# Scales for the up weights found unit by unit, the second norm's weight applied at the transposed eviction, two surveys moved

## The chip, the core and the metric

The kernel runs on one core of a Trainium2 chip. That core has a matrix engine (TensorE, PE in the rows), three engines for elementwise work (VectorE or DVE, ScalarE or ACT, GpSimd or POOL), and SyncE (SP), which here does little but issue transfers. Each engine works through its own queue in order; they meet by semaphores. The metric is the device time of one execution in microseconds (us).

## The reference

The kernel computes one layer of an encoder on 1024 positions of width 1024, in fp32:

```python
h = layer_norm(x, ln_in_w, ln_in_b)
h = layer_norm(DN_ALPHA * h + hybrid_mixer(h, ...), ln1_w, ln1_b)
h = layer_norm(DN_ALPHA * h + memory_xattn(h, mem, w_xq, w_xkv, w_xo, b_xo), ln2_w, ln2_b)
h = layer_norm(DN_ALPHA * h + conv_ffn(h, w_up, b_up, w_dw, b_dw, w_down, b_down), ln3_w, ln3_b)
```

`hybrid_mixer` is one input projection, a bidirectional chunked mLSTM on half of its columns and a neighbourhood attention on the rest, and an output projection. `memory_xattn` attends from each position to 256 memory tokens in four heads. `conv_ffn` multiplies by `w_up` (1024 x 5632) and adds `b_up`, applies a depthwise convolution of width 3 over positions, gates one half of the columns with the GELU of the other, and multiplies by `w_down` (2816 x 1024).

## The kernel before

**Numbers.** Each fp32 operand of a matmul is split into an f16 high and an f16 low part, and `mm3` (L217 to L219) adds three matmuls: high with high and the two mixed ones. So that the parts fit f16's range, an operand is first multiplied by a power of two. For a weight that power comes from a *survey*: the matrix is loaded once just to be measured (`survey_gen`, L194 to L206: an Abs on ScalarE with a running sum at L205, for a few pieces a maximum on VectorE at L203), `scale_of` (L168 to L177) folds the sums into one number for all partitions with a small matmul (the bank `mx`, L174) and `pow2` makes the power of two and its inverse. Later the weight is loaded again, piece by piece, and split by `split16` (L189 on ScalarE, L190 on VectorE). The survey of `w_up` is 44 loads of 512 KB, that of `w_down` 11 of 1 MB, those of `w_xo` and `w_xq` four of 1 MB each.

**Stages**, with their places in the profiled span. *Stage A* (0 to 200 us): input norm, and the columns of the input projection that are wanted with positions on partitions (`tk`, L323); its loop steps the surveys of `w_down`, `w_xo`, `w_xq`. *Mixer* (200 to 640): the other columns, mLSTM and neighbourhood attention. *Output projection and first norm* (640 to 690): `out_half` makes one tile of 128 positions after the other, `after1` (L928 to L936) normalises it, stores it to `h1_d`, steps the survey of `w_up` and, three tiles later, `to_T16` transposes it into f16 operands. `ln_tile` (L226 to L244) is the norm: VectorE statistics, GpSimd power (L235), ScalarE (r - mean)/std (L241), VectorE times weight (L242), GpSimd plus bias (L243). *Cross-attention* (690 to 900): queries (`xq`), then per head scores `S`, softmax (L1039 to L1044: maximum, difference, exponential, sum, normalisation), transposes of the probabilities (L1047), `PTh`/`PTl` and `pv`; between its steps, queries of later heads and the survey. *Second projection and norm* (840 to 955): `out_d` loads the residual tile `r` (`load_r`, which also adds `b_xo / ALPHA` on GpSimd, L1094), adds the projection, normalises, stores to `h2_d`; `to_B` (L982 to L1010) transposes it with TensorE (L989) and makes the f16 operands of the feed-forward: B11, B21, B22 and the sums T1 to T4. *Feed-forward up* (1000 to 1440): 22 units of 256 columns, gate and value half, each seven products of 12 matmuls in place of eight (a Strassen scheme): A11, A12, A22 and sums S1 to S4 of the unit's weight blocks against B and T. `Units.load` and `prep` bring and split a unit two units ahead, into one of four *homes* (buffers named `unitYh`, `unitYl`, `unitA`, `whi`/`wlo` in the rows) by the one scale `su`. `take` (L1267) empties a product's bank: m1, u2, u3, C21 by ScalarE with the bias, C11, C22, C12 by VectorE adding a kept piece. `post` (L1242) does convolution, GELU, gate and the store. *Down projection and third norm* (1360 to 1625).

**What sets the order.** All engines' queues are laid out ahead by the tile framework, which simulates the program on a timeline and picks the next instruction; within a queue nothing overtakes. SyncE issues nearly all loads and stores, one after the other, and a load whose buffer isn't free yet holds those behind it. Buffers of one name rotate in program order. The few lines on the old survey of `w_up`:

```python
survey = survey_gen(sv, [(I["w_up"][i // 2, :, i % 2 * 1024:i % 2 * 1024 + 1024], i) for i in range(2 * NFF)])
...
run(survey)
pu, su = scale_of(sums[:, 0:2 * NFF], 13)
```

## Time and profile before

| What | Value |
|---|---|
| three timed runs | 1631.69, 1631.81, 1634.49 us; median 1631.81 |
| profiled execution | 1627.17 us, span 1625.5 us |
| TensorE busy | 1503.0 us, 92% of the span |
| VectorE, ScalarE, GpSimd busy | 973.4, 753.2, 544.6 us |
| moved by DMA | 226.69 MB, mean 139 GB/s |

The profile is of one execution. The rows are of these kinds. A *window* gives, for a stretch of the span, each engine's busy time with its count of instructions, then TensorE's granted clock as a share of full speed (PEclk), the busy share of the DMA engines and what they moved. A *wait* row names who waited for whom, the total, how often, and the longest. A *group* row gives line, engine, operation, output and inputs, shapes, the count, busy time and mean ns of one, then the engine's idle time before them and what ended it. A *timeline* row gives start, duration, the instruction and, in brackets, the idle time before it and what ended that. `SPq` is the queue of loads and stores.

### The profile page before, as it was taken

To read this page: it belongs to the slowest core of one execution; us is meant where nothing else is said; L and a number is where in the kernel's file an instruction comes from. 1 tells how busy PE (TensorE), PEld (TensorE's weight loads), DVE (VectorE), ACT (ScalarE), POOL (GpSimd) and SP (SyncE) were. 2 spreads that over 40 slices of the span, in tenths; PEclk is the share of its full clock that TensorE was granted. 3 is DMA by queue.
4 is the path that set the end of the run, shared out by engine and by line. 5 is a ranking of instruction groups with operands and counts; after the bars stand their busy time and mean duration, and the time that the engine had idled before them with its cause. 6 is when DMAs were issued, how large, how long until landed. Compare 5 with 4: busy or idle time off the path is not lost.

```text
span 1625.5 us, 21513 instructions
## 1 busy us (share of the span) xinstructions
PE 1503.0 (92%) x8112; PEld 975.5 (60%) x8112; DVE 973.4 (60%) x1719; ACT 753.2 (46%) x1258; POOL 544.6 (34%) x372
## 2 busy tenths in 40 slices
PE   6998999999888989797789968999999999999997
PEld 5998888889777878644345533444444444444443
DVE  7411611237578885767566786887777676835333
ACT  3335201225555765656654444656665655622111
POOL 5414222114457761322002546454345410010133
PEclk9999999999999999898989978999999999999999
DMA  8278511266556325777631313222222232741112
GB/s 299 91 270 299 172 52 59 97 169 177 161 163 214 132 79 187 254 261 255 220 130 39 114 68 107 84 98 91 99 83 78 91 130 78 281 146 53 62 55 78
DMA packets 80377, 226.69 MB, mean 139 GB/s; under 512 B 7824, under 2 KB 26512, under 8 KB 76048
## 3 DMA queue, kind: packets, MB, share of 16 engines
q1 hardware_dynamic: 80128, 224.82, 40.3%
q8 instruction: 64, 1.05, 0.3%
q0 software_dynamic: 144, 0.49, 0.2%
q14 instruction: 41, 0.34, 0.1%
HBM read 182.71 MB, written 43.06 MB: 139 GB/s over the span
## 4 chain that ended last, share of the span: by engine, by line
PE 59%; DMA 12%; DVE 9%; ACT 6%; POOL 5%; issue 4%; SPq 0%; POOLq 0%; ACTq 0%; DVEq 0%
PE z L217 7%; PE z L218 7%; PE z L219 7%; PE dn L218 4%; PE dn L219 4%; PE dn L217 4%; DMA sv<-in_w_up_dram 4%; PE cl L217 4%; PE cl L219 4%; PE cl L218 4%; DMA whi<-mrow 2%; DMA mo<-ev 1%; ACT sv L205 1%; DMA r<-h 1%; PE o L863 1%
## 5 line engine op out<-in xcount | busy, mean ns | idle before, releaser
L127 POOL TENSOR_TENSOR wlo<-wraw,whi 128x1024 fp32r<-128x1024 f32 (+1 forms) x36 | 86.8, 2416 | 193.6 <-ACT whi L126 184.2
L190 DVE SCALAR_TENSOR_TENSOR wlo<-wraw,sc,whi 128x1024 f16<-128x1024 f32 x67 | 87.8, 1319 | 83.8 <-ACT whi L189 83.6
L217 PE MATMUL dn<-whi,yp 128*128 128x512 f16 x336 | 127.2, 379 | 0.0
L218 PE MATMUL dn<-wlo,yp 128*128 128x512 f16 x336 | 127.2, 379 | 0.0
L219 PE MATMUL dn<-whi,yp 128*128 128x512 f16 x336 | 126.9, 379 | 0.0
L189 ACT ACTIVATE whi<-wraw,sc 128x1024 f16<-128x1024 f32 x67 | 75.8, 1144 | 105.4 <-PE dn L219 46.3
L235 POOL TENSOR_TENSOR lnrs<-lnrs,mhalf 128x1 f32<-128x1 f32 x32 | 26.3, 822 | 283.9 <-DVE lnrs L234 161.6
L126 ACT ACTIVATE whi<-wraw 128x1024 fp32r<-128x1024 f32 (+1 forms) x48 | 50.4, 1056 | 121.8 <-PE cl L218 75.4
L205 ACT ACTIVATE sv<-sv 128x1024 f32<-128x1024 f32 (+1 forms) x55 | 70.9, 1289 | 71.8 <-DMA sv<-in_w_down_dram 38.3
L1173 POOL TENSOR_TENSOR wraw<-ur 128x512 f32<-128x512 f32 x22 | 41.2, 1873 | 156.1 <-DVE wlo L190 73.6
L243 POOL TENSOR_TENSOR r<-r,vec 128x1024 f32<-128x1024 f32 x22 | 51.8, 2356 | 77.5 <-DVE r L242 69.4
L1434 POOL TENSOR_TENSOR r<-r,vec 128x1024 f32<-128x1024 f32 x8 | 19.0, 2376 | 158.2 <-ACT r L1433 158.2
L1250 DVE SCALAR_TENSOR_TENSOR cbuf<-C,wdw,cbuf 128x1024 f32<-128x1024 f32 x44 | 70.7, 1607 | 1.1
L217 PEld LDWEIGHTS <-whi 128*128 128x128 f16 x364 | 36.3, 100 | 56.5 <-issue 16.5
L1249 DVE SCALAR_TENSOR_TENSOR cbuf<-C,wdw,cbuf 128x1024 f32<-128x1024 f32 x44 | 63.7, 1448 | 7.7 <-ACT cbuf L1248 6.7
L218 PEld LDWEIGHTS <-whi 128*128 128x128 f16 x364 | 36.2, 99 | 47.7 <-issue 7.7
L219 PEld LDWEIGHTS <-wlo 128*128 128x128 f16 x364 | 36.1, 99 | 45.1 <-issue 3.6
L217 PE MATMUL tk<-whi,X2h 128*128 128x256 f32 (+1 forms) x192 | 56.2, 292 | 6.5 <-DVE ev L323 5.2
L1248 ACT ACTIVATE cbuf<-C,bdw,wdw 128x1024 f32<-128x1024 f32 x44 | 54.4, 1236 | 12.2 <-DVE C L1286 11.4
L219 PEld LDWEIGHTS <-yp 128*128 128x128 f16 x352 | 34.4, 98 | 41.5
L217 PEld LDWEIGHTS <-yp 128*128 128x128 f16 x352 | 34.4, 98 | 41.5
L218 PEld LDWEIGHTS <-yp 128*128 128x128 f16 x352 | 34.4, 98 | 41.4
(444 smaller groups left out, 4850.9 us busy)
## 6 DMA issues: line engine op xcount, KB each, us to landing
sv<-in_w_up_dram SPq DMA_DIRECT2D x44, 512.0 KB
ur<-in_w_up_dram SPq DMA_DIRECT2D x22, 1024.0 KB
r<-h SPq DMA_DIRECT2D x23, 512.0 KB
sv<-in_w_down_dram SPq DMA_DIRECT2D x11, 1024.0 KB
y<-cbuf SPq DMA_DIRECT2D x22, 512.0 KB
ur<-y SPq DMA_DIRECT2D x11, 1024.0 KB
wraw<-in_w_down_dram SPq DMA_DIRECT2D x22, 512.0 KB
wraw<-in_w_col_dram SPq DMA_DIRECT2D x16, 512.0 KB
```

Source lines behind the costliest of these rows:

```text
L126: A.activation(hi[:, :n], r3, AF.Copy)
L127: (eng or G).tensor_tensor(lo[:, :n], r3, hi[:, :n].bitcast(F32), OP.subtract)
L189: A.activation(hi, src, AF.Copy, scale=s)
L190: V.scalar_tensor_tensor(lo, src, s, hi, op0=OP.mult, op1=OP.subtract)
L205: A.activation(t, t, AF.Abs, accum_out=sums[:, i:i + 1])
L217: T.matmul(ps, lh, rh, start=first, stop=False, skip_group_check=skip)
L218: T.matmul(ps, lh, rl, start=False, stop=False, skip_group_check=skip)
L219: return T.matmul(ps, ll, rh, start=False, stop=last, skip_group_check=skip)
L243: G.tensor_tensor(r, r, b_t, OP.add)
L1248: A.activation(c, C[:, 1:SEQ + 1], AF.Identity, scale=wdw[:, 1, j:j + 1], bias=bdw[:, j:j + 1])
L1249: V.scalar_tensor_tensor(c, C[:, 0:SEQ], wdw[:, 0, j:j + 1], c, op0=OP.mult, op1=OP.add)
L1250: V.scalar_tensor_tensor(c, C[:, 2:SEQ + 2], wdw[:, 2, j:j + 1], c, op0=OP.mult, op1=OP.add)
```

## The change

Line numbers of the changed kernel differ from those above; both stand in the rows below.

1. The survey of `w_up` is gone: 44 loads, 40 Abs and 4 maxima. In its place each unit is measured from the copy that is loaded anyway: `bound` runs one Abs over its 128 x 2048 values (output dumped into the unit's own home, sum kept), `scale` folds the sums with one bf16 matmul into `mx`, a reduction and four tiny VectorE operations. The unit's scale `c` is then applied where a product leaves its bank (`take`), so m1, u2, u3 are written straight into the convolution's buffers `C`, and VectorE's additions become (product x c + piece).
2. The survey of `w_down` leaves stage A. It becomes 22 loads of 512 KB, written in the source inside the feed-forward loop (`survey_down`), into two buffers that hold the second norm's weight and bias before. In stage A the other eight loads come at every fourth tile.
3. The second norm's weight and bias no longer pass through `ln_tile` (no L242, L243 for its eight tiles; for the last tile one VectorE operation in place of two). They are applied in `to_B` at the transposed eviction, where a column of 128 is one partition's constant: eight ScalarE operations of 128x128 with scale and bias columns (`wb2`) in place of two of 128x512. The stored residual is without them; the end stage multiplies and adds them there.
4. `b_xo / ALPHA` is added on GpSimd in the first norm's stage (`to_h1`, after the transposes, before the store to `h1_d`), no longer in `load_r`.
5. At the end `r` is scaled and shifted by two GpSimd operations instead of one ScalarE and one GpSimd.
6. Unit 0 is prepared after the second step of the second half of `out_d`, part of unit 1 (A11, A12, A22) between its tiles, the rest of unit 1 in the loop's first round.

The core of the diff:

```diff
+    def amax_all(am, b, idt):
+
+        pb = bank("mx")[:, :128]
+        T.matmul(pb, bass.AP(tensor=am.tensor, offset=am.offset, ap=[am.ap[0], [0, 128]]), idt, start=True, stop=True)
+        V.tensor_reduce(b, pb, axis=mybir.AxisListType.X, op=OP.max)
...
+        if late and w_t is None:
+            return V.tensor_scalar(r, r, mv[:, 0:1], rs[:, 0:1], op0=OP.subtract, op1=OP.mult)
...
-                survey = survey_gen(sv, [(I["w_down"][g], 22 + g) for g in range(NFF // 2)] + [
+                survey = survey_gen(sv, [
                     (I["w_xo"][256 * i:256 * i + 256].rearrange("(a p) c -> p a c", a=2), 33 + i) for i in range(4)] + [
-                    (I["w_xq"][2 * i:2 * i + 2].rearrange("i p k c -> p i (k c)"), 16 + i) for i in range(4)])
+                    (I["w_xq"][2 * i:2 * i + 2].rearrange("i p k c -> p i (k c)"), 16 + i) for i in range(4)], range(16, 20))
...
-                        if tt % 2 == 0 or c > 3:
+                        if tt % 4 == 0:
...
-        survey = survey_gen(sv, [(I["w_up"][i // 2, :, i % 2 * 1024:i % 2 * 1024 + 1024], i) for i in range(2 * NFF)])
...
+            bxo = vec(2, "b_xo")
+            V.tensor_scalar(bxo, bxo, 1.0 / ALPHA, None, op0=OP.mult)
+
+            def to_h1(tt, r):
+                to_T16(r, h1, tt, s1)
+                G.tensor_tensor(r, r, bxo, OP.add)
+                S.dma_start(h1_d[tt * 128:(tt + 1) * 128, :], r)
...
-                next(survey, None)
                 rq.append((tt, r))
                 if len(rq) > LAG:
-                    t_, r_ = rq.pop(0)
-                    to_T16(r_, h1, t_, s1)
+                    to_h1(*rq.pop(0))
...
+            B1 = B1s[:, tt // 2]
+            if tt % 2:
+                dst = [r[:, i * 512:i * 512 + 512].rearrange("p (k t) -> p k t", k=4) for i in range(2)]
+            else:
+                dst = [B1[:, q] for q in range(2)]
+            for q in range(2):
+                for k in range(4):
+                    i = 4 * q + k
+                    A.activation(dst[q][:, k], pts[q][:, k], AF.Identity, scale=wb2[:, i:i + 1], bias=wb2[:, 8 + i:9 + i])
...
-                    A.activation(B1[:, q, :, o], pts[q], AF.Copy, scale=sh)
-                    A.activation(Bh[:, 0, q, :, o], B1[:, q, :, o], AF.Copy)
-                    V.tensor_tensor(Bh[:, 1, q, :, o], B1[:, q, :, o], Bh[:, 0, q, :, o], OP.subtract)
+                    A.activation(Bh[:, 0, q, :, o], B1[:, q], AF.Copy)
...
-            A.activation(e12, pts[0], AF.Copy, scale=sh)
-            A.activation(e22, pts[1], AF.Copy, scale=sh)
+            e12, e22 = dst
...
+            wb2 = small.tile([128, 16], F32, name="wb2")
+            S.dma_start(wb2, I["ln2_c"])
+            V.tensor_scalar(wb2, wb2, sh, None, op0=OP.mult)
...
-                    G.tensor_tensor(rs[tt], rs[tt], bxo, OP.add)
...
-        run(survey)
-        pu, su = scale_of(sums[:, 0:2 * NFF], 13)
...
+            def bound(self, v):
+
+                if v < NFF:
+                    self.am[v] = ur.tile([128, 1], BF, name="am", tag="am", bufs=3)
+                    l1 = ur.tile([128, 1], F32, name="l1", tag="l1", bufs=3)
+                    A.activation(self.home(v)[1].bitcast(BF), self.raw[v], AF.Abs, accum_out=l1)
+                    V.tensor_copy(self.am[v], l1)
+
+            def scale(self, v):
+                if v < NFF:
+                    b = ur.tile([128, 4], F32, name="us", tag="us", bufs=5)
+                    self.s[v] = b[:, 2:3], b[:, 3:4]
+                    amax_all(self.am.pop(v), b[:, 0:1], identb)
+                    pow2(b[:, 0:1], 14, (b[:, 1:2], b[:, 2:3]))
...
+        out_d2 = out_d(range(4, NT), "out", 1)
+        next(out_d2)
+        units.bound(0)
+        units.bound(1)
+        next(out_d2)
+        units.scale(0)
+        units.scale(1)
         run(units.prep(0))
-        out_d2 = out_d(range(4, NT), "out", 1)
-        for _ in range(9):
+        for _ in range(4):
             next(out_d2)
-        run(units.prep(1))
         units.load(2)
+        prep1 = units.prep(1, True)
+        next(prep1)
+        for _ in range(3):
+            next(out_d2)
+        next(prep1)
         run(out_d2)
+        units.bound(2)
...
-                    A.activation(m1, X[v], AF.Identity, bias=bg)
+                    A.activation(g0, j4(X[v]), AF.Identity, scale=c, bias=bg)
                 elif what == "C11":
-                    V.tensor_tensor(g0, j4(Z[v]), j4(m1), OP.add)
+                    V.scalar_tensor_tensor(g0, j4(Z[v]), c, g0, op0=OP.mult, op1=OP.add)
...
+            def survey_down(i):
+
+                t = sv[i % 2]
+                S.dma_start(t, I["w_down"][i // 2, :, i % 2 * 1024:i % 2 * 1024 + 1024])
+                A.activation(t, t, AF.Abs, accum_out=dsum[:, i:i + 1])
...
+                units.scale(v + 2)
...
+                if v < NFF - 1:
+                    survey_down(v)
+                    if v == 0:
+                        survey_down(NFF - 1)
+                units.bound(v + 3)
...
-                A.activation(r, r, AF.Copy, scale=al)
-                G.tensor_tensor(r, r, bd, OP.add)
+                G.tensor_tensor(r, r, rw, OP.mult)
+                G.tensor_tensor(r, r, rb, OP.add)
```

**SyncE's queue in the first norm.** Before, survey loads (`sv<-in_w_up`) stand between the residual's loads and stores and the query weights (`wraw<-in_w_xq`):

```order
L730 DMA r<-part_73 128x1024 x4
L199 DMA sv<-in_w_up_dram 128x1024 x3
L930 DMA h_74<-r 128x1024
L199 DMA sv<-in_w_up_dram 128x1024 x2
L730 DMA r<-part_73 128x1024
L930 DMA h_74<-r 128x1024
L199 DMA sv<-in_w_up_dram 128x1024 x3
L930 DMA h_74<-r 128x1024
L199 DMA sv<-in_w_up_dram 128x1024 x2
L133 DMA wraw<-in_w_xq_dram 128x1024
```

Of the change, from the same place on to the start of cross-attention:

```order
L934 DMA h_74<-r 128x1024
L133 DMA wraw<-in_w_xq_dram 128x1024 x2
L1030 DMA wraw<-xk 128x2x256
L934 DMA h_74<-r 128x1024
L1031 DMA wraw<-xv 128x2x256
L1030 DMA wraw<-xk 128x2x256
L1031 DMA wraw<-xv 128x2x256
L934 DMA h_74<-r 128x1024 x2
L114 DMA vec_7858<-in_ln_w_dram 128x1024
L934 DMA h_74<-r 128x1024
L1325 DMA sv_9201<-in_w_down_dram 128x1024
L114 DMA vec_7860<-in_ln_b_dram 128x1024
```

No survey load is left in the first norm. All 22 of `w_down` (L1325) follow from here on, though the source has them in the feed-forward loop: their buffers are free once the second norm's weight and bias have been measured.

**TensorE between the second projection and the feed-forward** (`out`: the projection's products; `tp`: transposes of the normalised tiles; `z`: feed-forward products). Before, eight transposes stand well inside the projection, and sixteen behind its last matmul:

```order
L219 MATMUL out<-whi,pYl 128x512
L989 MATMUL tp<-ident,r 128x128 x8
L217 LDWEIGHTS pYl
...
L219 MATMUL out<-whi,pYl 128x512
L989 MATMUL tp<-ident,r 128x128 x16
L217 LDWEIGHTS unitYh
L217 MATMUL z<-Bh,unitYh 128x512
```

Of the change:

```order
L219 MATMUL out<-whi,pYl 128x512
L172 LDWEIGHTS am
L172 MATMUL mx<-identb,am 128x128
L993 MATMUL tp<-ident,r 128x128 x40
L217 LDWEIGHTS unitYh
L217 MATMUL z<-Bh,unitYh 128x512
```

The transposes of five tiles (3 to 7) now stand together behind the last matmul, after unit 1's `mx`.

**ScalarE behind the projection, of the change** (L1169: Abs of a unit; L193: split of a unit; L1003: evictions of transposes with the norm's weight and bias; L1019: f16 copies of T operands):

```order
L1169 ACTIVATE unitYl,l_9103<-ur 128x2048
L1003 ACTIVATE r<-tp,wb_7868 128x128 x8
L193 ACTIVATE unitA<-ur,us 128x1536
L1003 ACTIVATE Bf<-tp,wb_7868 128x128 x3
L1019 ACTIVATE TX1l<-wraw 128x4x128
```

Before, tile 3's evictions were two operations and no Abs stood ahead of them.

116 lines of the change are left out of this document (57 added, 59 removed).

## The prediction

> **What bounds the kernel now.** I read the page first: busy shares, then the chain that ended last.
>
> ```profile
> PE 1503.0 (92%) x8112; PEld 975.5 (60%) x8112; DVE 973.4 (60%) x1719; ACT 753.2 (46%) x1258; POOL 544.6 (34%) x372
> PE z L217 7%; PE z L218 7%; PE z L219 7%; PE dn L218 4%; PE dn L219 4%; PE dn L217 4%; DMA sv<-in_w_up_dram 4%; PE cl L217 4%; PE cl L219 4%; PE cl L218 4%; DMA whi<-mrow 2%; DMA mo<-ev 1%; ACT sv L205 1%; DMA r<-h 1%; PE o L863 1%
> ```
>
> TensorE is busy for 1503.0 of 1625.5 us, so a change that leaves its matmuls alone can win at most its 122.5 us of idleness and what the reduced clock costs. The chain names a removed transfer: the survey of `w_up` holds 4% of it (some 65 us, much of which other work would hold in its stead), and its Abs (L205) 1%. The next view, ten-microsecond windows, tells where TensorE loses.
>
> ```profile
> core 0: us, PE busy (x) PEld busy (x) DVE busy (x) ACT busy (x) POOL busy (x), PEclk, DMA share, GB/s
> 150.00:160.00 10.00, 8.14 (x68) 7.72 (x66) 2.06 (x9) 5.65 (x8) 4.89 (x5) 1.00 0.97 329
> 160.00:170.00 10.00, 6.03 (x28) 6.03 (x29) 6.11 (x18) 2.84 (x4) 1.54 (x2) 0.50 0.85 308
> 680.00:690.00 10.00, 3.00 (x11) 2.00 (x12) 6.80 (x11) 7.50 (x12) 0.55 (x1) 0.61 0.87 291
> 700.00:710.00 10.00, 7.33 (x30) 3.34 (x29) 7.64 (x11) 6.20 (x9) 1.99 (x3) 0.83 0.83 263
> 730.00:740.00 10.00, 4.03 (x19) 2.45 (x18) 8.64 (x16) 7.12 (x14) 2.41 (x2) 0.67 0.94 363
> 740.00:750.00 10.00, 5.95 (x28) 3.95 (x28) 9.73 (x20) 4.23 (x12) 6.88 (x3) 0.67 0.52 210
> 770.00:780.00 10.00, 4.64 (x30) 2.96 (x29) 4.99 (x9) 6.75 (x14) 0.00 (x0) 0.89 0.80 263
> 960.00:970.00 10.00, 3.06 (x14) 2.39 (x13) 8.65 (x11) 5.17 (x6) 5.52 (x3) 0.50 0.25 100
> 970.00:980.00 10.00, 7.31 (x19) 2.47 (x19) 9.56 (x13) 4.00 (x7) 6.12 (x3) 0.54 0.19 67
> 1059.00:1240.00 181.00, 181.00 (x840) 82.09 (x839) 143.38 (x114) 108.76 (x122) 85.03 (x42) 1.00 0.24 88
> ```
>
> Ten units of the feed-forward loop (last row, 18.1 us each) leave TensorE no gap at full clock: nothing can be won there, only lost. The losses that this change touches lie at four places: around 160 us (end of stage A), 680 to 710 (tail of the first norm), 730 to 780 (start of cross-attention) and 955 to 1000 (second norm into the feed-forward). Third view, waits:
>
> ```profile
> PE tk L217 <- DVE ev L323: 5.2, 1, 5.2
> ACT sv L205 <- DMA sv<-in_w_up_dram: 27.1, 20, 3.7
> SPq L199 <- ACT sv L205: 67.8, 32, 7.1
> PE tp L989 <- POOL r L243: 10.0, 2, 6.0
> PE pv L217 <- ACT PTh L189: 6.1, 2, 5.4
> ```
>
> The second and third rows (640 to 850 us) are head-of-line blocking both ways: ScalarE stands 27.1 us for survey data with norm and softmax work queued behind, and the load queue stands 67.8 us for ScalarE with real loads behind.
>
> **The change part by part**, against the profiled execution's own 1627.17 us.
>
> *Stage A.* 11 of 19 MB of surveys leave. The `tk` wait of 5.2 us is for an eviction whose buffer a store still held, at a moment with the DMA at 0.97. The windows 150 to 170 lack 1.86 + 3.97 = 5.8 us of matmul, and 6.03 us at clock 0.50 cost 3.0 more. With 8 MB left the queue has room: I take −6; bounds 0 (the other 8 MB fill it as well) and −9.
>
> *Tail of the first norm, 680 to 710.* In 680 to 690 and 700 to 710, 7.0 + 2.7 us are idle, and clocks of 0.61 and 0.83 cost 1.2 + 1.2. The last tiles' norm stands behind surveys on ScalarE:
>
> ```profile
> 677.81 1.06 ACT L205 ACTIVATE sv<-sv 128x1024 f32<-128x1024 f32 x1 [1.96 <-DMA sv<-in_w_up_dram]
> 681.52 1.04 ACT L205 ACTIVATE sv<-sv 128x1024 f32<-128x1024 f32 x1
> 683.13 1.05 ACT L205 ACTIVATE sv<-sv 128x1024 f32<-128x1024 f32 x1
> 686.77 1.15 ACT L189 ACTIVATE whi<-wraw,sc 128x1024 f16<-128x1024 f32 x1 [2.50 <-DMA wraw<-in_w_xq_dram]
> ```
>
> Three Abs with a wait of 1.96 make 5.1 us, and the weight that comes 2.50 us late was queued behind survey loads. All go: 7.6 us, plus a third of the clock's loss: −9. Bounds −13 (idleness and clock whole) and −4. The eight `b_xo` adds that move into this stage are on GpSimd, which has room (0.55 of 10 in the window 680 to 690); what they may do to VectorE is a rival below.
>
> *Start of cross-attention, 730 to 750.* The removed adds of `load_r` ran here, and VectorE's smallest work waited for them:
>
> ```profile
> 737.59 9.29 POOL L1094 TENSOR_TENSOR r<-r,vec 128x1024 f32<-128x1024 f32 x4 [14.28 <-DMA r<-h]
> 738.34 1.68 DVE L1040 TENSOR_TENSOR mn<-mn,sc 128x1 f32<-128x1 f32 x2
> 740.00 2.25 DVE L1040 TENSOR_TENSOR mn<-mn,sc 128x1 f32<-128x1 f32 x1
> 742.42 2.26 DVE L1044 TENSOR_SCALAR P<-P,mn 128x256 f32<-128x256 f32 x1
> 744.79 2.25 DVE L1044 TENSOR_SCALAR P<-P,mn 128x256 f32<-128x256 f32 x1
> 747.62 0.27 DVE L1040 TENSOR_TENSOR mn<-mn,sc 128x1 f32<-128x1 f32 x2
> 748.33 0.35 DVE L1044 TENSOR_SCALAR P<-P,mn 128x256 f32<-128x256 f32 x1
> ```
>
> The last two rows show the same operations undisturbed. The four slow rows exceed them by 1.4 + 2.1 + 1.9 + 1.9 = 7.3 us, on the softmax chain for which TensorE waits (10.0 us idle in the two windows). With a little of the clock's 3.3 us: −8; bounds −12 and −2 (the first scores wait for their operands anyway).
>
> *Rest of cross-attention.* The moved survey of `w_down`, 22 loads of 512 KB, lands exactly here by the order of the load queue, where 21 of `w_up` stood. Each costs ScalarE the same 1.05 us. So the 5.4 us wait for `PTh` and the window 770 to 780 largely stay: −2; bounds −8 and +4 (blocking at another softmax step).
>
> *Second norm into the feed-forward.*
>
> ```profile
> 959.12 1.97 PE L989 MATMUL tp<-ident,r 128*128 128x128 f32 x8 [3.98 <-POOL r L243]
> 972.08 0.58 PE L217 MATMUL z<-Bh,unitYh 128*128 128x512 f16 x1 [2.99 <-ACT Bh L994]
> 994.29 0.58 PE L218 MATMUL z<-TX1l,unitYh 128*128 128x512 f16 x1 [1.78 <-DVE TX1l L1010]
> 443.53 1.28 ACT L538 ACTIVATE whi<-whi,g_sb 128x128 f32<-128x128 f32 x4 [3.06 <-DMA whi<-mrow]
> L189 ACT ACTIVATE unitA<-ur,sc 128x1536 f16<-128x1536 f32 x6 | 9.4, 1565 | 1.8 <-PE z L218 1.8
> L205 ACT ACTIVATE sv<-sv 128x2048 f32<-128x2048 f32 x15 | 28.7, 1914 | 44.5 <-DMA sv<-in_w_down_dram 38.3 <-DMA sv<-in_w_xo_dram 6.2
> L1009 ACT ACTIVATE TX1h<-wraw 128x512 f16<-128x512 f32 x8 | 4.9, 624 | 3.8 <-DVE wraw L1006 2.0 <-DVE wraw L1004 1.8
> L993 ACT ACTIVATE Bf<-tp,sc 128x512 f32<-128x512 f32 x8 | 5.1, 679 | 1.6 <-PE tp L989 1.6
> ```
>
> Now: the projection ends at 959.12 − 3.98 = 955.1, the first feed-forward product starts 16.9 later, and the T-operand products run for good from 994.3, 39 later. After: the GpSimd add and the multiply leave the norm, but the order puts the transposes of tiles 3 to 7 behind the last projection matmul, and an eviction becomes eight pieces: 2 × 1.28 = 2.6 us a tile for 2 × 0.68. ScalarE then does, in its queue's order up to the first B operand, an Abs (1.9 + 0.2 for its read-out), tile 3 (2.6), a split (1.6), tiles 4 to 6 (7.7), nine T copies between them (9 × 0.62) and three f16 copies (3 × 0.68): 21.6, less some 0.09 by which neighbours overlap (four of 0.39 took 1.28) on a dozen of them: 20.5 us to the first product, 3.6 later than now. The 48 B products take 48 × 0.216 = 10.4 (181.0 us for 10 × 84 gives 0.216), and with a third of them at half clock, as now, 14: to 34.5. The T operands of the last tile are done within that. So 35 to 37 against 39, and 1.7 less in the projection, whose last sixteen transposes moved out (8 took 1.97 at the reduced clock): −5. Bounds: −13 (the waits of 10.0 and half the clock) and +6 (evictions at 0.39 us a piece instead of 0.32, with the T operands behind them).
>
> *Feed-forward loop.* Per unit: one more matmul, one more Abs and a little on VectorE.
>
> ```profile
> L174 PE MATMUL mx<-ident,sc x16: 271/275/275, 365.5 to 1477.9; 128*128 128x128 f32 x16
> ```
>
> ScalarE has 108.76/10 = 10.9 us a unit and gets 2.1 more, VectorE 14.3 and about 1 more (six tiny operations; the scaled evictions are the same in number and size): both stay under 18.1. On TensorE 22 matmuls of at most 0.27 us, whose form is cheaper than this f32 one: +2; bounds +1 and +6. A cover gone is the slower rival.
>
> *End.* The scaled residual becomes two GpSimd operations of 2.4 us for a ScalarE one and one:
>
> ```profile
> L1434 POOL TENSOR_TENSOR r<-r,vec 128x1024 f32<-128x1024 f32 x8 | 19.0, 2376 | 158.2 <-ACT r L1433 158.2
> ```
>
> GpSimd stood idle 158 us around its eight; 19 more hide under the projection: 0; bounds 0 and +2.
>
> **Sum:** −6 − 9 − 8 − 2 − 5 + 2 + 0 = −28, 1599 for the profiled execution. The median lies 4.6 above it (1631.81): **1604**.
>
> **Rivals.**
> *The blocking moves with the survey.* The queue order speaks for it: 22 loads, two buffers, in-order Abs between softmax steps. Then cross-attention gains nothing (8 + 2 lost) and its delay eats the junction's 5: 1631.8 − 6 − 9 + 2 = 1619. Against it: the four rows at 738 to 747 owe nothing to a survey.
> *The lock moves with the add.* Eight adds of 2.6 us enter the first norm's stage. If each holds VectorE for 2.1, as the row at 740.00 did, that is 17 us of VectorE in a stage where this row has it busy 32 of 50:
>
> ```profile
> sum 50.00, PE 40.36 PEld 32.71 DVE 32.24 ACT 27.54 POOL 12.28; mean PE 8.07 PEld 6.54 DVE 6.45 ACT 5.51 POOL 2.46
> ```
>
> (640 to 690.) It would be full, and the gain of 9 gone: 1613. The Trainium skill (SBUF — State Buffer, section "SBUF: two separate sides") states a mechanism for this: a GpSimd operation and a VectorE operation with two SBUF inputs exclude each other for the whole instruction. The rows at 738 and 740 agree (two-input L1040); the one-SBUF-input L1044 at 742.42 was held as well, which that sentence alone allows only in a fast mode. Against the rival, without the page: a held VectorE hurts only on the last two tiles, before them the projection covers it.
> *More goes.* Without both causes cross-attention's start and the idleness at 770 vanish whole, each term at its good bound but the loop: 1631.8 − 9 − 13 − 12 − 8 − 13 + 2 ≈ 1579.
> *Slower: the loop falls out of step.* The Abs writes its dump into the next unit's buffer, so in ScalarE's queue it waits until TensorE has left that buffer; behind it stand u3's and the next m1's evictions, for which the product's PSUM bank waits. Between m1 and the product's next use lie 24 matmuls, 5.2 us. If the Abs makes m1 later than that, by 1.6 us say (a wait of 4.7 and its 2.1), 22 units pay 35: 1604 + 35 = 1639. Against: 7 us a unit free on ScalarE; for: one strict queue.
>
> **How the numbers follow.** Forecast 0.57, own range 1592 to 1615; blocking moves 0.18; the lock 0.08; more goes 0.08; out of step 0.06; the parts cancel 0.03. Range 1579 to 1624, which leaves out the last two and little more. 0.2% (3.3 us) is about what a measurement tells from no change: faster 0.57 + 0.18 + 0.08 + 0.08 = 0.91, same 0.03, slower 0.06.
>
> **What would show it.** Stage A: no `tk` wait near 160 and a clock of 1.00. First norm: 680 to 690 with TensorE above 6. Cross-attention: L1050 and L1054 (the softmax lines now) at 0.15 to 0.5 us; Abs (L1325) waits on ScalarE of 10 us and more mean the blocking rival. Junction: one long TensorE wait of 17 to 21 us before the first `z` and a second product group without its 4.5. Loop: 18.1 to 18.3 us a unit. A unit above 18.5, or POOL adds (L933) beside 2 us DVE rows after 675, would make me wrong.

## The result, and the profile after

| | Before | Changed |
|---|---|---|
| median of the timed runs | 1631.75 us (1629.98 to 1634.49) | 1615.32 us (1612.37 to 1616.35) |
| ratio, 95% interval | 1 | 0.9895 (0.9876 to 0.9914) |
| profiled execution, span | 1627.17, 1625.5 us | 1615.6, 1613.9 us |

The change makes the kernel faster: by 1.05% by the ratio, whose interval leaves out 1, and by 16.4 us between the medians. 1604 was forecast, 27.8 us less. The two profiled executions lie 11.6 us apart, since that of before was 4.6 us faster than its median and that of after was not; the account below is made between the two profiles.

First the page of the changed kernel (engines, then the lines of the chain that ended last):

```profile
PE 1497.6 (93%) x8132; PEld 969.9 (60%) x8132; DVE 980.9 (61%) x1836; ACT 763.9 (47%) x1284; POOL 544.8 (34%) x373
DVE cbuf L1284 4%; DVE cbuf L1285 3%; DVE wlo L194 2%; DMA sv<-in_w_down_dram 2%; PE z L217 2%; PE out L217 2%; PE z L219 2%; PE z L218 2%; PE out L219 2%; PE out L218 2%; DMA r<-h 2%; ACT whi L193 1%; POOL r L247 1%; DVE unitYl L194 1%; POOL r L1486 1%
```

The survey of `w_up` has left the chain; in its place stand a survey again (that of `w_down`) and VectorE's convolution steps of the feed-forward loop. The windows, at the places of the prediction:

```profile
160.00:170.00 10.00, 8.98 (x75) 8.72 (x74) 9.09 (x21) 1.17 (x3) 2.22 (x3) 1.00 0.40 134
670.00:680.00 10.00, 3.14 (x19) 2.70 (x18) 9.64 (x11) 4.72 (x7) 6.66 (x2) 0.81 0.44 157
720.00:730.00 10.00, 1.27 (x6) 0.49 (x5) 4.76 (x10) 4.30 (x9) 2.35 (x1) 0.70 0.64 199
730.00:740.00 10.00, 4.70 (x24) 3.05 (x24) 4.82 (x13) 6.99 (x14) 0.00 (x0) 0.62 0.92 343
950.00:960.00 10.00, 4.79 (x18) 3.19 (x19) 7.27 (x10) 10.00 (x27) 2.75 (x3) 0.50 0.00 0
1079.00:1264.60 185.60, 182.56 (x844) 81.00 (x843) 153.68 (x172) 127.96 (x141) 78.85 (x40) 1.00 0.23 85
```

The hole at 160 us is nearly closed. The hole in the first norm's tail is still there (now at 670, 3.14 us of matmul where 3.00 was), and at the start of cross-attention TensorE does 1.27 + 4.70 us of work in 20. The last row holds ten units of the feed-forward loop: they take 185.6 us, not 181.3. What TensorE waits for (640 to 760 us, then 1010 to 1480):

```profile
PE S L217 <- ACT kh L193: 11.9, 1, 11.9
PE tp L266 <- POOL r L247: 6.9, 1, 6.9
...
PE mx L172 <- DVE am L1170: 2.5, 4, 0.8
```

In the profile of before (640 to 760 us) the wait for `kh` is 2.4 us, the first norm's tail waits for something else, a step of its statistics, and there is no wait for a unit's `mx`:

```profile
PE tp L262 <- DVE lnrs L234: 5.3, 1, 5.3
PE S L217 <- ACT kh L189: 2.4, 1, 2.4
```

To see what each is worth, the span was cut at first and last starts of groups of matmuls, whose amount of work the change hardly alters (`cl`: the mixer's first products; `od` and `out`: the second projection's, of the first and the second half of the positions):

| Stretch on TensorE, us | before | changed | difference | forecast |
|---|---|---|---|---|
| start to first `cl` (stage A) | 178.9 | 171.8 | −7.1 | −6 |
| to last mixer output product (mixer) | 499.4 | 498.9 | −0.5 | 0 |
| to first `od` (first norm's tail, cross-attention) | 167.7 | 161.9 | −5.8 | −19 (9 + 8 + 2) |
| to last `out` of the second projection | 108.8 | 106.8 | −2.0 | −1.7 |
| to last `z` with `TX1l` (junction and loop) | 426.3 | 427.2 | +0.9 | −1.3 |
| to the end | 244.4 | 247.3 | +2.9 | 0 |
| sum | 1625.5 | 1613.9 | −11.6 | −28 |

Behind the last `z` with `TX1l` 24 more `z` products follow, among the first products of the down projection. One line of the table carries most of the error: 13 us of the 19 that the first norm and cross-attention should have given did not come.

### The profile page after: what moved, and what is told of

The parts are those of the page before. It is cut to its first block, busy times and chain, and to the rows that moved or that the text cites. A ratio compares the mean times of both kernels' runs of the same rounds, so it can differ in the third digit from the quotient of the medians.

```text
span 1613.9 us, 21573 instructions
## 1 busy us (share of the span) xinstructions
PE 1497.6 (93%) x8132; PEld 969.9 (60%) x8132; DVE 980.9 (61%) x1836; ACT 763.9 (47%) x1284; POOL 544.8 (34%) x373
## 3 DMA queue, kind: packets, MB, share of 16 engines
q8 instruction: 64, 1.05, 0.3%
## 4 chain that ended last, share of the span: by engine, by line
DVE 22%; PE 20%; ACT 11%; issue 9%; DMA 9%; POOL 6%; POOLq 0%; SPq 0%; ACTq 0%; DVEq 0%
DVE cbuf L1284 4%; DVE cbuf L1285 3%; DVE wlo L194 2%; DMA sv<-in_w_down_dram 2%; PE z L217 2%; PE out L217 2%; PE z L219 2%; PE z L218 2%; PE out L219 2%; PE out L218 2%; DMA r<-h 2%; ACT whi L193 1%; POOL r L247 1%; DVE unitYl L194 1%; POOL r L1486 1%
## 5 line engine op out<-in xcount | busy, mean ns | idle before, releaser
L1203 POOL TENSOR_TENSOR wraw<-ur 128x512 f32<-128x512 f32 x22 | 44.6, 2028 | 195.0 <-issue 184.2
L243 ACT ACTIVATE r<-r,lnrs 128x1024 f32<-128x1024 f32 x22 | 27.3, 1240 | 148.7 <-DVE lnrs L242 148.7
L1284 DVE SCALAR_TENSOR_TENSOR cbuf<-C,wdw,cbuf 128x1024 f32<-128x1024 f32 x44 | 77.2, 1754 | 26.6 <-ACT cbuf L1283 26.5
L194 DVE SCALAR_TENSOR_TENSOR wlo<-wraw,sc,whi 128x1024 f16<-128x1024 f32 x45 | 65.2, 1462 | 45.3 <-ACT whi L193 45.3
L193 ACT ACTIVATE whi<-wraw,sc 128x1024 f16<-128x1024 f32 x45 | 51.0, 1144 | 66.7 <-PE dn L219 25.8
L1285 DVE SCALAR_TENSOR_TENSOR cbuf<-C,wdw,cbuf 128x1024 f32<-128x1024 f32 x44 | 70.8, 1610 | 1.2
L1486 POOL TENSOR_TENSOR r<-r,vec 128x1024 f32<-128x1024 f32 x8 | 19.8, 2475 | 129.9 <-DMA r<-h 129.9
L217 PE MATMUL tk<-whi,X1h 128*128 128x256 f32 (+1 forms) x192 | 55.9, 292 | 1.9 <-DVE V L322 1.1
```

Source lines behind the costliest of these rows:

```text
L193: A.activation(hi, src, AF.Copy, scale=s)
L194: V.scalar_tensor_tensor(lo, src, s, hi, op0=OP.mult, op1=OP.subtract)
L217: T.matmul(ps, lh, rh, start=first, stop=False, skip_group_check=skip)
L1203: G.tensor_tensor(S1, A21, A22, OP.add)
L1284: V.scalar_tensor_tensor(c, C[:, 0:SEQ], wdw[:, 0, j:j + 1], c, op0=OP.mult, op1=OP.add)
L1285: V.scalar_tensor_tensor(c, C[:, 2:SEQ + 2], wdw[:, 2, j:j + 1], c, op0=OP.mult, op1=OP.add)
```

## The experiments

Each experiment's kernel is compared with the kernel before by its ratio, and with the changed kernel by the stretches above. In the table, "norm and attention" is the third stretch, "junction and loop" the fifth. Stretches are of one profiled execution each. Kernels with the same code in norm and attention agree there within 2.2 us (161.0 to 162.8; 152.2 and 153.9; 141.2 to 143.4). The mixer, which no experiment edits, takes 494.2 to 500.7 us, so spans say less than stretches. In the two kernels with the later `mx`, 48 and not 24 `z` products follow behind the fifth stretch.

| Kernel | Ratio to before (95%) | norm and attention | junction and loop | span |
|---|---|---|---|---|
| changed | 0.9895 (0.9876 to 0.9914) | 161.9 | 427.2 | 1613.9 |
| late survey | 0.9879 (0.9861 to 0.9896) | 152.2 | 428.5 | 1607.3 |
| no survey of `w_down` | 0.9865 (0.9849 to 0.9882) | 155.6 | 429.1 | 1606.3 |
| `b_xo` add back | 0.9877 (0.9862 to 0.9892) | 153.9 | 429.1 | 1606.8 |
| no unit scale | 0.9898 (0.9875 to 0.9922) | 161.0 | 417.7 | 1607.4 |
| before without survey of `w_up` | 0.9889 (0.9864 to 0.9914) | 147.9 | 426.2 | 1607.1 |
| late survey, late residual loads | 0.9826 (0.9805 to 0.9848) | 143.4 | 428.5 | 1597.6 |
| cast on ScalarE | 0.9921 (0.9896 to 0.9946) | 162.0 | 430.5 | 1613.3 |
| late survey, dump elsewhere | 0.9806 (0.9785 to 0.9826) | 153.9 | 415.7 | 1594.6 |
| later `mx` | 1.0148 (1.0124 to 1.0172) | 162.8 | 465.0 | 1653.1 |
| three repairs | 0.9729 (0.9709 to 0.9749) | 141.2 | 417.1 | 1586.7 |
| three repairs, later `mx` | 0.9951 (0.9934 to 0.9968) | 142.1 | 451.7 | 1622.2 |
| three repairs, bf16 sums | 0.9800 (0.9776 to 0.9825) | 143.1 | 427.1 | 1595.9 |

### The new wait at the start of cross-attention

Two theories for the 11.9 us: the moved survey's Abs stand ahead of the split of k on ScalarE (A), or the moved adds hold SyncE's stores, and the loads of k behind them (B). ScalarE's timeline in the changed kernel:

```profile
719.12 1.06 ACT L1326 ACTIVATE sv<-sv 128x1024 f32<-128x1024 f32 x1 [3.19 <-DMA sv<-in_w_down_dram]
723.87 1.06 ACT L1326 ACTIVATE sv<-sv 128x1024 f32<-128x1024 f32 x1 [2.44 <-DMA sv<-in_w_down_dram]
726.88 1.06 ACT L1326 ACTIVATE sv<-sv 128x1024 f32<-128x1024 f32 x1 [1.28 <-DMA sv<-in_w_down_dram]
731.12 1.06 ACT L1326 ACTIVATE sv<-sv 128x1024 f32<-128x1024 f32 x1 [3.10 <-DMA sv<-in_w_down_dram]
732.43 0.72 ACT L193 ACTIVATE kh<-wraw,sc 128x512 f16<-128x512 f32 x1 [0.15 <-issue]
```

Four surveys wait 10.0 us in all for their transfers, and the split of k (`kh`), for which TensorE waits, stands behind them. *Late survey*: the 22 loads are tied to the loads of the units.

```diff
-                    survey_down(v)
-                    if v == 0:
-                        survey_down(NFF - 1)
+                    with tc.issue_after(units.last.ins):   # the DMA of the last unit loaded
+                        for i in range(NFF):
+                            if 3 + i * 18 // NFF == v:
+                                survey_down(i)
```

> The changed kernel with one difference: the 22 survey loads of w_down are held in SyncE's queue behind the loads of the up units, so they run in the feed-forward loop and not in cross-attention. In the changed kernel's trace TensorE waits 11.9 us for kh at the start of cross-attention; four survey Abs (719 to 732 us, 10.0 us of waits for their transfers) stand ahead of that split on ScalarE, though k landed some 30 us before. Theory A (blocking moved with the survey): the wait falls to 2 us or less, the first scores start 10 to 12 us earlier against the matmuls before them, the kernel is 10 us or more faster than the changed one (about 1604). Theory B (GpSimd's moved b_xo adds hold the stores in SyncE's queue, 37.2 us, and so k): the wait stays above 8 us and the time within 4 us of 1615. The loop has 22 more Abs of 1.25 us on ScalarE (of some 5 us free a unit): under A no more than 2 us over all units.

Measured: 0.9879, and 152.2 us from the last mixer output product to the first `od`, 9.7 less. The first scores start 17.5 us behind the last `xq` product in place of 24.4. TensorE's wait for k, and the split of k on ScalarE's timeline:

```profile
PE S L217 <- ACT kh L193: 5.0, 1, 5.0
...
723.71 0.72 ACT L193 ACTIVATE kh<-wraw,sc 128x512 f16<-128x512 f32 x1 [3.49 <-DMA h<-r]
```

Neither theory came as forecast; each has its part. Seven of the 11.9 us went with the surveys. Of the 5.0 that are left the profile puts 3.49 on a store of `h1_d` (issued at 720.72 us), which waits for a moved add, B's cause. But k's loads had been issued by 694.0 us, so it isn't the load that is held: the split waits for the store itself. That its output lies where the first norm's tiles were is read from the source and not shown. The time fell less than A said, and by the ratios alone the two kernels can't be told apart (0.9879 and 0.9895, intervals overlapping). Part of what was won is lost behind the loop, where the last stretch takes 251.7 us and not 247.3. There the survey ends late (its last piece in the 21st unit), `w_down`'s scale with it, and TensorE waits 2.7 us for a split of `w_down`. *No survey of `w_down`* leaves it out altogether:

> The changed kernel without any survey of w_down: a constant stands for its sums, the survey's loads and Abs are left out. Theory A: the same start of cross-attention as with the late survey, and a time within 3 us of it, since Abs in the loop are covered; what it is faster than the late survey by is the price of Abs in the loop. Theory B: within 4 us of the changed kernel's 1615.

Measured: 0.9865, and 155.6 and 429.1 us, so 22 Abs in the loop cost nothing that can be seen there (428.5 with them). TensorE's wait for k is 5.9 us, so what the late survey leaves of it isn't the survey's.

### The moved add

TensorE's wait of 6.9 us for `r` at the first norm's tail, seen from GpSimd's and TensorE's timelines of the changed kernel:

```profile
672.07 3.38 POOL L933 TENSOR_TENSOR r<-r,vec 128x1024 f32<-128x1024 f32 x1 [2.87 <-PE tp L266]
675.41 3.32 POOL L247 TENSOR_TENSOR r<-r,vec 128x1024 f32<-128x1024 f32 x1
...
678.78 1.97 PE L266 MATMUL tp<-ident,r 128*128 128x128 f32 x8 [6.86 <-POOL r L247]
```

The `b_xo` add of an earlier tile (L933) waits 2.87 us for that tile's transposes, runs 3.38 us, and the norm's own bias add (L247) of the tile that TensorE needs stands behind it. *Add back*: `to_h1` stores without the add, `load_r` adds as before.

```diff
-                G.tensor_tensor(r, r, bxo, OP.add)            # to_h1
                 S.dma_start(h1_d[tt * 128:(tt + 1) * 128, :], r)
...
                     S.dma_start(rs[tt], h1_d[tt * 128:(tt + 1) * 128, :])
+                    G.tensor_tensor(rs[tt], rs[tt], bxo, OP.add)   # load_r
```

> The changed kernel with the b_xo add back in load_r (at the start of cross-attention) instead of the first norm. The prediction's reading (VectorE's small softmax steps are held by the GpSimd adds for 7.3 us): slow rows of 1.7 to 2.3 us return at the first softmax steps and the stretch from the first scores to the first pv (11.7 us in the changed kernel, 24.4 before) grows by 5 to 8 us. Theory B: the kh wait of 11.9 goes as well, and the time stays or falls. Under theory A the wait stays and the kernel is 4 to 8 us slower than the changed one (1619 to 1623).

Measured: from the last mixer output product to the first `xq` 2.4 us where the changed kernel has 10.0, so the add cost 7.6 us there. As expected, the stretch from the first scores to the first `pv` grew, from 11.7 to 21.8 us, since five adds in a row came back beside the first softmax steps:

```profile
712.10 12.87 POOL L1104 TENSOR_TENSOR r<-r,vec 128x1024 f32<-128x1024 f32 x5 [9.18 <-DMA r<-h]
712.65 2.77 DVE L194 SCALAR_TENSOR_TENSOR kl<-wraw,sc,kh 128x512 f16<-128x512 f32 x1
715.41 2.76 DVE L194 SCALAR_TENSOR_TENSOR vl<-wraw,sc,vh 128x512 f16<-128x512 f32 x1
718.09 2.31 DVE L1087 TENSOR_SCALAR wb<-wb,sc 128x16 f32<-128x16 f32 x1
722.94 2.11 DVE L1049 TENSOR_TENSOR mn<-mn,sc 128x1 f32<-128x1 f32 x2
```

A 128x16 operation of VectorE takes 2.31 us beside these adds (0.23 in the changed kernel). I had expected 4 to 8 us more than the changed kernel if the surveys alone held k; it is as fast as the late survey (0.9877), because the scores start so much earlier (712.0 against 733.2) that the slow steps are paid for. The wait for k is gone here, though the surveys are where they were: with the stores early, the splits of k stand ahead of the first survey on ScalarE. So the 11.9 us can't be shared out between survey and add. Taking the survey away removes 6.9 of them, taking the add away all.

*Before without the survey of `w_up`* does the change's first part alone, with a constant in place of the sums:

```diff
-        survey = survey_gen(sv, [(I["w_up"][i // 2, ...], i) for i in range(2 * NFF)])
+        survey = iter(())
+        V.memset(sums[:, 0:2 * NFF], 26.0)
```

> The kernel before with one thing left out: the survey of w_up (44 loads, 44 measurements); a constant stands for its sums. It prices the removed part alone. If the survey's loads and Abs were what the first norm's tail and cross-attention lost (the prediction's reading of the waits 27.1 and 67.8 us): from the last mixer output matmul to the last xq matmul 9 us less (40.3 before), the window 770 to 780 full, 15 to 25 us less in all, about 1605 to 1613 where before is 1629. Rival: the GpSimd adds at the start of cross-attention and the junction set the pace, and these loads are covered: under 8 us, above 1621. The stretch from the first scores to the first pv stays above 20 us in both cases (24.4 before), since the adds are still there.

Measured: 0.9889, as much as the whole change gives, and 19.8 us less in norm and attention alone (from the first scores to the first `pv` 19.5 us, where above 20 was expected). So the survey was the blocker that it was taken for, and its price is in the range expected here. The place was wrong: from the last mixer output product to the last `xq` this kernel takes 38.1 us, as the changed kernel does (40.3 before), and not 31. The reason is the same add: with the survey gone the residual loads come sooner, the framework runs four of the adds in the first norm, and the same wait opens:

```profile
681.81 2.34 POOL L1095 TENSOR_TENSOR r<-r,vec 128x1024 f32<-128x1024 f32 x1 [3.65 <-DMA r<-h]
684.11 3.32 POOL L243 TENSOR_TENSOR r<-r,vec 128x1024 f32<-128x1024 f32 x1
687.48 1.97 PE L262 MATMUL tp<-ident,r 128*128 128x128 f32 x8 [6.70 <-POOL r L243]
```

*Late survey, late residual loads* takes the adds out of both places: back in `load_r`, whose loads now stand in SyncE's queue behind those of `w_xo`.

```diff
-                    S.dma_start(rs[tt], h1_d[tt * 128:(tt + 1) * 128, :])
+                    with tc.issue_after(xo_ld[min(tt, 7)].ins):    # the load of one piece of w_xo
+                        S.dma_start(rs[tt], h1_d[tt * 128:(tt + 1) * 128, :])
+                    G.tensor_tensor(rs[tt], rs[tt], bxo, OP.add)
```

> The late survey and the b_xo add back in load_r, but with the loads of the residual tiles held in SyncE's queue behind those of w_xo, so that the adds come in the middle of cross-attention. Theory A (adds in the first norm hold the norm's own GpSimd work and cost 7.6 us there; adds at the first scores cost 10 us there; surveys ahead of the k split cost 10 us): all three go, the first norm's tail as with the add in load_r (2.4 us from the last mixer output matmul to the first xq), first scores to first pv 10 us, and 8 to 12 us less than the late survey alone: ratio to before 0.980 to 0.983. Rival (the adds cost the same wherever they run): a new TensorE wait of 5 us or more in the middle of cross-attention and a time within 3 us of the late survey.

Measured: 0.9826; norm and attention 143.4 us, 8.8 less than with the late survey alone, 18.5 less than changed, 24.3 less than before. From the last mixer output product to the last `xq` it is now 30.9 us, 9.4 less than before. The first five adds run at 773 to 798 us, where the longest wait of TensorE is 4.5 us: the cost of an add depends on who stands behind it. One expectation missed: from the first scores to the first `pv` it takes 19.3 us and not 10, since 24 products for the queries of later heads (`fill`) now stand between them.

### The price of a scale for each unit

*No unit scale*: one constant for all units; the Abs and the folding matmul of each unit are left out.

```diff
-                    A.activation(self.home(v)[1].bitcast(BF), self.raw[v], AF.Abs, accum_out=l1)
-                    V.tensor_copy(self.am[v], l1)
...
-                    amax_all(self.am.pop(v), b[:, 0:1], identb)      # every unit
+                        V.memset(b[:, 0:1], 52.0)                    # once
```

> The changed kernel with one constant scale for all units: the Abs of each unit, its folding matmul and all but one set of tiny operations are left out; eviction with scale stays. It prices the per-unit measurement. My reading: 0.1 us a unit and some loop waits (about 4 us of TensorE idleness between 1080 and 1340) and 2 to 6 us at the junction, where Abs stand ahead of the evictions and the transposes of tiles 3 to 7 wait behind the second unit's mx: 5 to 10 us faster than the changed kernel (1605 to 1610). If the transposes still stand together behind the last projection matmul, the dump into the home isn't what holds them. Rival: Abs and mx are covered, and the scaled evictions into C make the loop's waits: then within 2 us of 1615.

Measured: 0.9898, no faster than the changed kernel, where 5 to 10 us less were expected. Both prices show all the same. At the junction the first T product comes 23.4 us behind the last `out` and not 32.8. In the loop ten units take what they took before (181.3 us; the changed kernel 185.6):

```profile
1079.00:1260.30 181.30, 181.30 (x842) 82.19 (x841) 141.78 (x112) 110.17 (x124) 88.97 (x40) 1.00 0.24 89
```

The evictions with scale are still in this kernel, so they aren't what lengthens a unit, and the rival falls: the 0.43 us a unit belong to the measurement (Abs, cast, fold and small operations together). The gain was spent in this kernel's own order: TensorE waits 4.7 us for an m1 eviction early in the loop, so junction and loop together give 9.5 us (417.7 against 427.2), and 3.9 us for a split of `w_down` behind it, where the last stretch takes 252.9 us against 247.3; the second projection takes 2.6 us more.

In the loop the price is at least in part a wait. A unit's m1 eviction comes every 18.56 us (1171.76, 1190.32), before every 18.13. In between, VectorE's and TensorE's timelines of the changed kernel (the last row is the load of the weights for `mx`):

```profile
1182.27 2.17 DVE L1285 SCALAR_TENSOR_TENSOR cbuf<-C,wdw,cbuf 128x1024 f32<-128x1024 f32 x1
1184.37 0.74 DVE L1320 SCALAR_TENSOR_TENSOR C<-z,us,C 128x512 f32<-128x512 f32 x1
1185.03 0.14 DVE L1170 CAST am<-l 128x1 bf16<-128x1 f32 x1
1185.22 0.10 PEld L172 LDWEIGHTS <-am 128*128 128x128 bf16 x1 [0.50 <-DVE am L1170]
```

The cast of the unit's sums takes 0.14 us, but it stands behind a convolution step and an eviction, and TensorE, in order, stands 0.50 us for it. *Cast on ScalarE* was to bring it forward:

```diff
-                    V.tensor_copy(self.am[v], l1)
+                    A.activation(self.am[v], l1, AF.Copy)
```

> The changed kernel with one small operation moved: the cast of a unit's sums to bf16 runs on ScalarE behind the Abs and not on VectorE, where it stands behind a convolution step of 2.2 us. In the changed kernel a unit takes 18.56 us against 18.13 before, and each mx matmul's weight load waits 0.5 us for that cast. If the wait is the price: 18.2 to 18.3 us a unit, 5 to 7 us less over 22 units, ratio to before 0.985 to 0.987. If the matmul itself is the price (a change of type or a drained pipeline): still above 18.45, and the time as the changed kernel's.

Measured: 0.9921, not faster than the changed kernel. The framework put the cast on ScalarE 4 us behind the Abs:

```profile
1179.90 0.19 ACT L1169 ACTIVATION_READ_ACCUMULATOR unitYl<-ur 128x1 f32 x1
1184.03 0.19 ACT L1170 ACTIVATE am<-l 128x1 bf16<-128x1 f32 x1
1184.27 0.10 PEld L172 LDWEIGHTS <-am 128*128 128x128 bf16 x1 [0.92 <-ACT am L1170]
```

The wait grew by 0.42 us (0.50 to 0.92), and the unit by 0.23, to 18.79. That the wait costs something follows; that it is all of the 0.43 does not.

*Later mx* moves the fold, and with it the first step of the unit's preparation, behind another product, so that the cast is long done:

```diff
-                units.scale(v + 2)
-                pr = units.prep(v + 2)
...
                 if v > 0:
-                    prod(X[v - 1], v - 1, "A22", "T4", False, True)
+                    pm = prod(X[v - 1], v - 1, "A22", "T4", False, True)
                     take(v - 1, "C21")
+                with tc.issue_after(pm.ins) if pm is not None else nullcontext():
+                    units.scale(v + 2)
+                pr = units.prep(v + 2)
```

> The changed kernel with one thing moved: a unit's folding matmul (mx) and scale are issued on TensorE behind the product A22 x T4 of the unit before last's round and not ahead of the round's first product, so that the cast which it needs has been done. If the wait for the cast is the loop's price (0.43 us a unit, and 0.66 where the cast came 0.4 us later): 18.2 us a unit, 6 to 8 us less over 22 units, ratio to before 0.985 to 0.987. If the scale now comes too late for the split of the next units, ScalarE's split waits show it and the unit stays at 18.5 or more.

Measured: 1.0148, slower than before. No `mx` waits any more, but the framework laid out the whole loop in another order, in which TensorE waits for the m1 eviction:

```profile
PE z L217 <- ACT C L1309: 29.7, 8, 3.7
```

Two units take 42.3 us (ten units 211.6 between VectorE's evictions at 1103.05 and 1314.65). This is the end that the slower rival of the prediction names (an m1 eviction too late for the product behind it), brought about by the repair and by another cause: in ScalarE's queue the eviction stands behind steps of `post` that wait for VectorE (L1292 3.13 us, L1289 0.70 us ahead of the eviction at 1185.31), not behind an Abs that waits for its buffer.

### The junction

*Late survey, dump elsewhere*: the first three units' Abs write their unused output into a free buffer and not into the unit's home.

```diff
-                    A.activation(self.home(v)[1].bitcast(BF), self.raw[v], AF.Abs, accum_out=l1)
+                    if v == 0:
+                        self.junk = vecs.tile([128, D], F32, name="junk", tag="vec0")
+                    dump = self.junk.bitcast(BF) if v < 3 else self.home(v)[1].bitcast(BF)
+                    A.activation(dump, self.raw[v], AF.Abs, accum_out=l1)
```

> The late survey, and the dump of the first three units' Abs goes to a free 4 KB buffer and not into their homes. By the built order the transposes of tiles 3, 4 and 5 then stand inside the projection and not behind its last matmul. If the dump into the home is what holds the junction: 5 to 8 us less from the last projection matmul to the T products (32.9 us with the late survey, 37.3 before), and so in all. Rival, borne out by the kernel without unit scales, where the first product came 13 us earlier and the end of the loop did not: ScalarE's evictions and T copies of the last tiles set the pace, and less than 2 us are won.

Measured: 0.9806; junction and loop 415.7 us against 428.5 with the late survey alone, 12.8 less, of which 11.3 lie between the last `out` and the first T product (21.4 against 32.7). More than expected; the rival falls. The block of forty transposes behind the last projection matmul came from that dump: the home of unit 1 is a buffer that `w_xo` holds until shortly before the projection ends, unit 1's `mx` waits for the Abs into it, and the transposes stand behind this `mx`.

### The three repairs together

Survey late, but two pieces a unit, so that its last piece comes in the 14th of the 22 units; residual loads late; dump elsewhere.

> The changed kernel with three repairs: the survey of w_down in the first half of the feed-forward loop (two pieces a unit), the b_xo adds back in load_r with the residual loads behind those of w_xo, and the first three Abs dumped into a free buffer. If the three costs are separate, they add: against the late survey alone the second gave 0.5 points of the ratio and the third 0.7, the late end of the survey in the down projection some 3 us: ratio 0.973 to 0.977, about 1587 where before is 1628. If they share a cause (one idle TensorE stretch counted twice), 0.979 or more.

Measured: 0.9729 (0.9709 to 0.9749), median 1586.85 us where before took 1630.0 in the same runs. The three repairs add up as expected for separate costs: norm and attention 141.2, junction and loop 417.1, from the last `z` to the end 247.2. It beats both kernels. The same with the later `mx`:

> The three repairs and the later mx together. If the mx wait is separate from them, 6 to 8 us less than the three alone: ratio 0.969 to 0.973, a unit of 18.2 us. If the later scale upsets the order of the loop, no faster than the three alone.

Measured: 0.9951: the order of the loop decides again (451.7 us). And the three repairs with sums that the Abs writes in bf16 at once, so that there is no cast of its own:

```diff
-                    A.activation(dump, self.raw[v], AF.Abs, accum_out=l1)
-                    V.tensor_copy(self.am[v], l1)
+                    A.activation(dump, self.raw[v], AF.Abs, accum_out=self.am[v])
```

> The three repairs, and the Abs writes its sums in bf16 at once, so that no cast on VectorE stands between a unit's Abs and its mx matmul. If the wait for the cast is the loop's price and the order of the loop stays in step: the waits of mx go, 18.2 to 18.3 us a unit, 5 to 7 us less than with the three repairs (ratio 0.969 to 0.971). If the framework's new order of the loop decides, as in the kernel with the later mx (PE waited 3.7 us at a time for the m1 eviction), the unit is 18.6 us or more, and the kernel slower than with the three repairs, though no mx waits.

Measured: 0.9800, slower than with the cast. Again the loop has another order. `mx` still waits, now for the Abs itself (2.7 us in all, 5.3 for the cast in the three repairs), and TensorE's waits for m1 reappear (first row; second, the three repairs alone; both 960 to 1340 us):

```profile
PE z L217 <- ACT C L1311: 9.5, 7, 2.2
```

```profile
PE z L217 <- ACT C L1312: 1.5, 1, 1.5
```

So what `mx` would cost without its wait in the order of the changed loop was not measured: each edit that freed it changed the order.

## Why the prediction was right, and where not

**Right.** The direction, the range (1579 to 1624 holds 1615.3), stage A (−6 forecast, −7.1), the second projection without its last sixteen transposes (−1.7 and −2.0), and the names of the three causes in norm and attention. Their sum was forecast at −19, and the kernel that has none of them there (late survey, late residual loads) has −24.3. The shares were off: leaving out the survey of `w_up` gave 19.8 us by itself, not 9 + 2. And that the median fell into the range is partly the range's width: 1615.3 lies just outside the forecast's own range (1592 to 1615), and 13 of the 28 us are missing at one place. The term for the first norm also adds up to 8.4 by its own numbers and was put at 9.

**The step that failed** is the one that let all three go at once: "All go: 7.6 us" in the first norm's tail, and "−8" at the start of cross-attention. Measured, the tail gave 0.2 us (10.2 to 10.0 from the last mixer output product to the first `xq`), and the start gave 5.2 us of idle time and lost 9.5 to the wait for k. Two of the three pieces of work were moved, not removed, and each went to a place with a queue behind it. This was on record as two rivals, at 1619 and 1613 with chances of 0.18 and 0.08, and priced apart from each other; each came true in part. Three signs that the prediction names for being wrong, or for the first rival, are there: waits of 10.0 us for the survey on ScalarE, a unit of 18.56 us, and POOL adds beside rows of VectorE of 2 us after 675:

```profile
681.69 2.64 DVE L194 SCALAR_TENSOR_TENSOR wlo<-wraw,sc,whi 128x1024 f16<-128x1024 f32 x1 [0.17 <-ACT whi L193]
```

- *The lock moves with the add.* "GpSimd, which has room" was read from the window 680 to 690 (0.55 of 10). Room was not the question: GpSimd works in order, and an add that waits for a transpose holds the norm of the next tiles. Price forecast 9 us; with the add back, 7.6 us less ahead of the first `xq`. The 8.0 of the whole stretch (161.9 to 153.9) is a balance: 12.1 more are won ahead of the first scores, 10.1 lost behind them, where the adds are again, and 1.6 elsewhere. Both mechanisms show: the queue (L933 ahead of L247) and the exclusion of VectorE (3.3 us for adds that take 2.4 alone). The Trainium skill's page SBUF — State Buffer (section "SBUF: two separate sides") names two SBUF inputs or a fast mode as the condition. In the add-back kernel a 128x16 `TENSOR_SCALAR` with one SBUF tensor took 2.31 us; by that sentence it must have run in a fast mode, which no run here shows.
- *The blocking moves with the survey.* Forecast as a loss in the middle of cross-attention, at the softmax steps; it came at its start, ahead of the split of k: 9.7 us (161.9 to 152.2), 6.9 of them ahead of the first scores. The moved add had a hand in it: with the add back, k isn't waited for at all. The order of SyncE's queue, which the prediction used, told where the loads stand; ScalarE's order at that place, where four Abs stand ahead of `kh`, would have told what they block, and was not used.

**The start of cross-attention itself** went as forecast in mechanism, and less far. From the first scores to the first `pv` 24.4 us became 11.7 (first row before, second changed):

```profile
732.60:757.00 24.40, 16.35 (x80) 9.79 (x80) 21.86 (x46) 14.49 (x31) 9.29 (x4) 0.72 0.65 249
733.20:744.90 11.70, 8.80 (x56) 6.24 (x56) 9.39 (x32) 8.35 (x22) 0.00 (x0) 0.81 0.97 374
```

But only 5.2 us of that is idle time (8.05 before, 2.90 now); the rest is 23 `fill` products that now stand further on. The softmax's small steps are undisturbed:

```profile
737.84 0.16 DVE L1050 TENSOR_TENSOR mn<-mn,sc 128x1 f32<-128x1 f32 x1
739.62 0.35 DVE L1054 TENSOR_SCALAR P<-P,mn 128x256 f32<-128x256 f32 x1
```

The wait of 11.9 us for k (2.4 before) took it back.

**Junction and loop.** Forecast −5 (1.7 of it in the second projection) and +2; measured +0.9 together. Ten units take 4.3 us more (185.6 and 181.3), so about 9 over the loop, and the junction gave about 8 by the difference. The loop's term was mis-sized: it priced `mx` by its own duration (0.27 us at most) and not by what it waits for, a cast in VectorE's queue; its own bound of +6 did not hold it. The junction's chain was worked out well (first product 20.5 us behind the projection forecast, 21.3 measured), but taken as given: the dump that forced it was not seen as its cause, though the prediction named that dump in its slower rival.

**The end**, forecast at 0 with +2 as its bound, lost 2.9 us behind the loop. Of these, 1.8 lie behind the last product of the down projection (11.1 us before, 12.9 now). For the last tile VectorE waits for the scaled residual, before until 1.4 us ahead of the start of that product, now until 0.2 us behind it:

```profile
1612.97 0.69 DVE L1436 TENSOR_TENSOR r<-r,half 128x512 f32<-128x512 f32 x1 [10.17 <-POOL r L1434]
1601.20 0.69 DVE L1489 TENSOR_TENSOR r<-r,half 128x512 f32<-128x512 f32 x1 [9.64 <-POOL r L1487]
```

So the second GpSimd operation isn't hidden on the last tile. The kernels with the old end have 11.1 and 11.3 us there, those with the new one 12.5 to 14.7. No experiment has changed the end alone, so this is a reading and not shown.

## What to carry to other kernels

A piece of work that leaves a critical place isn't gone until it is known what stands behind it at its new place, on every in-order queue that it passes: its loads, its engine, and the engine that it holds up while it runs. A tiny instruction (a cast of 0.14 us, a fold of 0.23) on a saturated engine costs what its inputs wait for, not what it takes. And where a scheduler lays out the loop, an edit of one line is an edit of the whole order, so look at the period of the loop before believing in the edit.

## What the runs showed that was not expected

Removing the survey of `w_up` alone moved other work without any edit: the residual loads rose in the queue, and their adds landed in the first norm, where they cost what the moved adds of the change cost (waits of 6.70 and 6.86 us). And three kernels that shortened or removed the wait for `mx` were slower in junction and loop than those with it: 465.0 us against 427.2 and 451.7 against 417.1 with the later `mx`, 427.1 against 417.1 with sums in bf16.
